# The opening of a hybrid attention encoder kernel: idle products first, half-size first loads, row scalings ahead of the squares, roots by square root and reciprocal

## The chip, the cores and the metric

The kernel runs on one core of a Trainium2 chip. The core has TensorE (PE, matrix products into PSUM), VectorE (DVE), ScalarE (ACT), GpSimd (POOL) and SyncE (SP), which here issues nearly all DMA transfers. Each engine takes its instructions in the order in which they were written to its queue and waits on semaphores for the others. The metric is the device time of one execution in microseconds (us); lower is better. The profile is one execution, recorded by the hardware; its span runs from the first to the last instruction.

## What is computed

One encoder layer is applied to 2048 prompt tokens and 512 sample tokens of width 1024, with 16 meta tokens ahead of each. What matters here is the beginning:

```python
def rms_norm(x, g):
    y = x32 * lax.rsqrt(jnp.mean(x32 * x32, axis=-1, keepdims=True) + RMS_EPS)
    return (y * g.astype(jnp.float32)).astype(x.dtype)

u = rms_norm(h, norm_g)
proj = u @ w_in                       # 1024 x 5376
qa, ka, va, za, qb, kb, vb, zb, ga, gb = jnp.split(proj, cuts, axis=-1)
# neighbourhood attention (a), windowed attention (b), gates, and
merged = jax.nn.sigmoid(ga) * y_a + jax.nn.sigmoid(gb) * y_b
return merged @ w_out                 # added to h, then a final rms_norm
```

Everything is float32. The kernel keeps that precision with three products of split operands: each operand is rounded to a high part (`fp32r`), the rest is the low part, and high x high, high x low and low x high are summed in PSUM (`mm3`, L146 to L148).

## The kernel before

The 2560 tokens are five windows of 512. Tokens lie along the free axis, the 1024 features along the 128 partitions in eight tiles. The opening projects the **last window** first, one weight tile (128 output features) at a time: 18 weight tiles in the list `firsts`, then the passes over pairs of windows follow. I call the 24 products (8 feature tiles x 3) of one weight tile a **group**; groups 1 to 4 make the queries of branch a, groups 5 to 8 those of branch b.

The projection needs only x times the norm's gain. The row factor, 1/sqrt(mean of squares), is a factor per token and is multiplied onto the group's result. So products can begin before the squares are summed. What the opening computes, by names that the profile shows:

- `wraw` is a weight tile as loaded, `wt` its high part (ACT, L207) and low part (VectorE, L208). Two buffers each.
- `xt` is a loaded pair of x tiles of the last window. `prep_last` scales it into the operand `u`: high part on ACT (L341), low part on VectorE (L342). It squares `xt` on ACT (L345) and sums the squares over the feature tiles into `rs` on VectorE (L347, L350). `xm` and `xms` are the same for the 16 meta tokens.
- `prep_last` is a generator. Its second part, the **row sums**, sums `rs` over the partitions with products against ones (`fin_v`, L368 and L369), takes the root (`rsqrt`, L151 to L164, an integer first guess and three Newton steps on VectorE) and writes it on a diagonal (`rs_dg`, L177). Its third part, the **spread**, turns the diagonal into a row factor on all partitions with products (`rs_rb`, L185), copied to `rs`.
- `prep_first` does the same for the first two windows (tiles `x`, squares `sq` at L426, sums `rsp` on POOL for one window, L428 and L431, and on VectorE for the other).
- `tq` and `evq` (L288, L253, L254) multiply a group's result by the row factor and split it; the query writes `qa<-evq` and `qb<-evq` go out by SP's queue. `zr` is a block of zeros that SP also writes out in between.

PE's and SP's order is that of the code (a manual schedule); ACT, VectorE and POOL are ordered by a scheduler, which may move instructions past each other, and the order is fixed when the program is built. `beside` runs the groups and counts the steps of each (a step is six products, four steps a group): the tuple `own` says after which steps the second and the third part of `prep_last` come, and the list `at` says after which steps `prep_first` goes on. A transfer that SP issues for `wraw` waits until the buffer's former tile has been split.

Of the kernel before, what the change touches and what calls it, by code (L numbers as in the profile page):

```python
# [9 lines left out]
F32 = mybir.dt.float32  # L10
# [85 lines left out]
def encoder_block(ctx: ExitStack, tc: tile.TileContext, xT, x_end, w_in, w_pa, w_pb, w_o, norm_g, final_g,  # L96
# [33 lines left out]
    ones = f32(ones_r)  # L130
    warm = const.tile([P, 1], F32, name="warm")
    nc.vector.memset(warm, 1.0)
    nc.scalar.activation(warm, warm, AF.Silu)
    ng = const.tile([P, KT], F32, name="ng")
    nc.scalar.dma_start(ng, norm_g)
    fg = const.tile([P, KT], F32, name="fg")
# [4 lines left out]
    def move(out, in_):  # L141
        last_move[0] = nc.sync.dma_start(*(f32(a) if a.dtype == F32R else a for a in (out, in_)))
        return last_move[0]
# [6 lines left out]
    def rsqrt(small, sq, m, nc_):  # L150

        ve, hv, r, t = (small.tile([P, 8], F32, tag=f"rs{i}", name=f"rs{i}")[:m, :nc_] for i in range(4))
        nc.vector.tensor_scalar(ve, sq, 1.0 / D_MODEL, EPS, ALU.mult, ALU.add)
        nc.vector.tensor_scalar(r.bitcast(I32), ve.bitcast(I32), 1, None, ALU.arith_shift_right)
        nc.vector.tensor_scalar(r.bitcast(I32), r.bitcast(I32), -1.0, float(0x5F3759DF), ALU.mult, ALU.add)
        nc.vector.tensor_scalar(hv, ve, -0.5, None, ALU.mult)
        for _ in range(3):
            if nc_ == 1:
                nc.vector.scalar_tensor_tensor(t, r, hv, r, ALU.mult, ALU.mult)
            else:  # L160
                nc.vector.tensor_mul(t, r, hv)
                nc.vector.tensor_mul(t, t, r)
            nc.vector.scalar_tensor_tensor(r, t, 1.5, r, ALU.add, ALU.mult)
        return r  # L164

    def sums(ssq, c0, m, nc_, psum, tag):
# [31 lines left out]
    def fetch_w(src):  # L198
        raw = wpool.tile([P, KT * P], F32, tag="wraw", name="wraw")
        if len(src.shape) == 3:  # L200
            move(raw.rearrange("p (a f) -> p a f", a=2), src.rearrange("a p f -> p a f"))
        else:
            move(raw, src)
        return raw
# [12 lines left out]
    class Weights:  # L217
# [16 lines left out]
        def next(self):  # L234
            i = self.i
            self.i += 1
            self.fetch(i + 2)
            self.split(i + 1)
            return self.wt.pop(i)
# [81 lines left out]

        return (up if i < 5 else uxp).tile(shape, F32R, tag=f"u{i}", name=name)

    def prep_last(meta):


        w = NWIN - 1
        uh, ul = (operand(i, [P, KT, PITCH], f"u4{i}") for i in (5, 6))
        us[w] = (uh, ul, us[w][2] if w in us else uxp.tile([P, UW + N_META], F32, tag="rs4", name="rs4")[:, :UW])
        rs = us[w][2]  # L330
        for k in range(0, KT, 2):
            rows = xT[k * P : (k + 2) * P]
            xt = ev.tile([P, 2, WTOK], F32, tag="ev", name="xt")
            move(xt, rows[:, w * WTOK : (w + 1) * WTOK].rearrange("(k p) t -> p k t", p=P))
            if meta and k == 0:
                xm = st.tile([P, KT, N_META], F32, tag="xm", name="xm", bufs=1)
                move(xm, xT[:, TOK:].rearrange("(k p) t -> p k t", p=P))
            for j in range(2):
                g = ng[:, k + j : k + j + 1]
                h = uh[:, k + j, :WTOK]  # L340
                nc.scalar.mul(h, xt[:, j, :], g)  # L341
                low[0] = nc.vector.scalar_tensor_tensor(ul[:, k + j, :WTOK], xt[:, j, :], g, f32(h), ALU.mult,  # L342
                                                        ALU.subtract).ins
            if meta:
                nc.scalar.activation(xt, xt, AF.Square)  # L345
                if k == 0:
                    nc.vector.tensor_add(rs[:, :WTOK], xt[:, 0, :], xt[:, 1, :])  # L347
                else:
                    for j in range(2):
                        nc.vector.tensor_add(rs[:, :WTOK], rs[:, :WTOK], xt[:, j, :])  # L350
        if not meta:
            return
        t = ev.tile([P, WTOK], F32, tag="t", name="xms", bufs=3)
        a, b = (t[:, i * P : (i + 1) * P].rearrange("p (k m) -> p k m", m=N_META) for i in range(2))
        nc.vector.tensor_mul(a, xm, ng[:, :, None].broadcast_to([P, KT, N_META]))
        mh, ml = uh[:, :, WTOK:UW], ul[:, :, WTOK:UW]
        nc.scalar.copy(mh, a)
        nc.vector.tensor_sub(ml, a, f32(mh))
        nc.scalar.activation(b, xm, AF.Square)
        for n in (4, 2):  # L360
            nc.vector.tensor_add(b[:, :n], b[:, :n], b[:, n : 2 * n])
        nc.vector.tensor_add(rs[:, WTOK:], b[:, 0], b[:, 1])
        yield
        sq = st.tile([P, 32], F32, tag="sq", name="sq", bufs=1)[:, :5]
        nc.vector.memset(sq, 1.0)
        v = ps_t.tile([P, WTOK], F32, tag="vt", name="fin_v")
        for c in range(4):
            nc.tensor.matmul(v[:, c : c + 1], rs[:, c * P : (c + 1) * P], ones[:, 0:1], start=True, stop=True)  # L368
        nc.tensor.matmul(v[:N_META, 4:5], rs[:, WTOK:], ones[:, 0:1], start=True, stop=True)  # L369
        nc.scalar.copy(sq[:, :4], v[:, :4])  # L370
        nc.scalar.copy(sq[:N_META, 4:5], v[:N_META, 4:5])
        r = rsqrt(uxp, sq, P, 5)
        dgs = [ev.tile([P, WTOK], F32, tag="t", name="rs_dg", bufs=3) for _ in range(2)]
        diagonal(dgs[0], r[:, :4], P)
        diagonal(dgs[1], r[:N_META, 4:5], N_META)
        yield
        for dg, c0, m, nc_ in (dgs[0], 0, P, 4), (dgs[1], WTOK, N_META, 1):
            nc.scalar.copy(rs[:, c0 : c0 + nc_ * m], spread(ps_t, "vt", dg, m, nc_)[:, : nc_ * m])
        yield
# [25 lines left out]
    def prep_first(sp, wa, loaded):  # L405
# [28 lines left out]
        for i in range(2):  # L434
            for c in range(4):
                nc.tensor.matmul(v[:, 4 * i + c : 4 * i + c + 1], rss[i][:, c * P : (c + 1) * P], ones[:, 0:1],
                                 start=True, stop=True)
        r = rsqrt(uxp, v[:, :8], P, 8)
        dgs = [ev.tile([P, WTOK], F32, tag="t", name="rs_dg", bufs=3) for _ in range(2)]
        for i in range(2):  # L440
            diagonal(dgs[i], r[:, 4 * i : 4 * i + 4], P)
# [557 lines left out]
    firsts = [*range(QA, KA), *range(QB, KB), *range(KA, ZA), KB, VB]  # L999
    rest = [f for f in range(GA) if f not in firsts]  # L1000

    def start_w(fs):
        raws = [fetch_w(w_in[f]) for f in fs[:1]]
        wts = [split_w(raws[0])]
        yield raws, wts
        raws.append(fetch_w(w_in[fs[1]]))
        raws.append(fetch_w(w_in[fs[2]]))
        yield
        wts.append(split_w(raws[1]))
        raws.append(fetch_w(w_in[fs[3]]))  # L1010
        yield
# [3 lines left out]
            pool = [pp.enter_context(tc.tile_pool(name=f"p{i}", bufs=1, reuse_waits="tile")) for i in range(3)]  # L1015
            return pairs(pool, wa, wa + 1, both, a, first.send(pool[2]), first, raw1, ahead, extra, opening)

    w0 = start_w(firsts)
    raws, wts = next(w0)
    own = prep_last(True)  # L1020
    next(own)
    with tc.tile_pool(name="sp", bufs=1, reuse_waits="tile") as sp:
        loaded = []
        steps = prep_first(sp, 0, loaded)
        next(w0)
        next(steps)
        next(w0)
        loaded.append(last_move[0])
        next(steps)
        zeros = zero_rows()  # L1030
        next(zeros)
        begun = beside(firsts, raws, wts, (own, (9, 14)), 0, steps, [2, 20, 27, *(28 + 27 * i // 10 for i in range(16))],
                       zeros)
    steps = [(0, 1), *((n, i) for n in range(1, KT) for i in (0, 1)), (KT, 0), (KT, 1), (KT, 2), (9, 1),
             *((j, i) for j in range(10, 18) for i in ((0, 2) if j % 2 == 0 else (1,)))]
# [777 lines left out]
```

## Time and profile before

| what | value |
|---|---|
| three runs | 1873.13, 1873.22, 1875.83 us; median 1873.22 |
| the profiled execution | 1874.68 us, span 1872.9 us |
| PE busy | 1851.8 us, 99% |
| VectorE, ACT, POOL busy | 70%, 61%, 42% |
| first product | 7.20 us after the span's start |
| mean granted TensorE clock | 0.999 |

The page's busy table gives each engine's share of the span. The table of waits says for which instruction of which engine an engine stood idle: total us, times, longest. A timeline row gives start, duration, engine, line, operation, what is written from what, its count and, in brackets, the idle time before it and what ended it. A row of a table of windows gives a stretch, its length, the busy time of PE, weight loads, VectorE, ACT and POOL with their instructions in brackets, the granted clock, the DMA engines' busy share and GB/s.

### The profile page before, as it was taken

What the parts mean: (1) busy time and instruction counts of PE and PEld (TensorE: products, weight loads), DVE (VectorE), ACT (ScalarE), POOL (GpSimd) and SP (SyncE); (2) the same over time, 40 slices, a digit from 0 to 9 for tenths busy, and PEclk for the clock granted to TensorE, in tenths of its full rate; (3) what the DMA queues carried; (4) which work ended last, traced back from release to release, by engine and by line L of the source; (5) the groups of instructions that cost most, each with busy time, mean ns of one, the idle gap of its engine ahead of it and who ended that gap; (6) DMA issues with size and microseconds to landing.
All of it is one profiled execution on the core that took longest, in us unless ns stands there. A gap on an engine that the chain in (4) does not pass through costs nothing. (4 is left out here: it accounts for less than half of the span.)

```text
span 1872.9 us, 29663 instructions
## 1 busy us (share of the span) xinstructions
PE 1851.8 (99%) x9755; PEld 1579.9 (84%) x9755; DVE 1317.6 (70%) x2914; ACT 1147.7 (61%) x2531; POOL 778.4 (42%) x599
## 2 busy tenths in 40 slices
PE   8999999999999999999999999999999999999998
PEld 6998888888888888888878888888888888888887
DVE  8986667556476556444457888878887887888874
ACT  6454444444365444444456797798789778878932
POOL 2015443323103232322324435647855865785420
PEclk9999999999999999999999999999999999999999
DMA  7665756645295677644259869968986998698473
GB/s 261 202 176 212 207 163 194 214 174 180 84 340 194 185 224 201 199 140 160 106 186 298 274 206 275 307 211 255 313 276 205 300 307 253 210 315 262 147 302 131
DMA packets 288145, 414.35 MB, mean 221 GB/s; under 512 B 117736, under 2 KB 162360, under 8 KB 286456
## 3 DMA queue, kind: packets, MB, share of 16 engines
q1 hardware_dynamic: 287704, 412.45, 68.9%
q8 instruction: 78, 1.28, 0.3%
q14 instruction: 75, 0.61, 0.1%
q10 hardware_dynamic: 288, 0.01, 0.0%
HBM read 303.46 MB, written 108.91 MB: 220 GB/s over the span
## 5 line engine op out<-in xcount | busy, mean ns | idle before, releaser
L208 POOL TENSOR_TENSOR wt<-wraw,wt 128x512 fp32r<-128x512 f32 x164 | 212.4, 1313 | 240.9 <-ACT wt L207 222.2
L868 PE MATMUL pa<-u,wt 128*128 128x512 f32 x1008 | 242.7, 389 | 0.2 <-DVE wt L208 0.2
L868 PE MATMUL pa<-u,x 128*128 128x512 f32 x984 | 236.5, 389 | 0.0
L207 ACT CAST wt<-wraw 128x512 fp32r<-128x512 f32 x312 | 177.8, 619 | 76.2 <-DMA wraw<-in_w_in_dram 29.8
L868 PEld LDWEIGHTS pa<-u,wt 128*128 128x128 f32 x1008 | 188.9, 188 | 39.8 <-DVE wt L208 0.6
L868 PEld LDWEIGHTS pa<-u,x 128*128 128x128 f32 x984 | 184.6, 188 | 38.4
L837 POOL TENSOR_TENSOR s<-wraw,raw 128x512 f32<-128x512 f32 x40 | 58.3, 1458 | 276.7 <-DVE x L208 276.7
L146 PE MATMUL mm<-u,wt 128*128 128x512 f32 (+2 forms) x416 | 150.2, 361 | 7.2 <-ACT u L341 7.2
L147 PE MATMUL mm<-u,wt 128*128 128x512 f32 (+2 forms) x416 | 146.8, 353 | 0.2 <-DVE u L342 0.2
L148 PE MATMUL mm<-u,wt 128*128 128x512 f32 (+2 forms) x416 | 146.7, 353 | 0.0
L208 DVE TENSOR_TENSOR wt<-wraw,wt 128x512 fp32r<-128x512 f32 x148 | 103.8, 738 | 53.5 <-ACT wt L207 53.4
L868 PE MATMUL pe<-u,wt 128*128 128x512 f32 x504 | 121.3, 390 | 0.0
L868 PE MATMUL pc<-u,wt 128*128 128x512 f32 x504 | 121.1, 389 | 0.0
L868 PE MATMUL pe<-u,x 128*128 128x512 f32 x480 | 115.3, 389 | 0.0
L842 POOL TENSOR_TENSOR s<-wraw,s 128x512 f32<-128x512 f32 x42 | 56.6, 1349 | 137.7 <-DVE wt L208 137.7
L868 PEld LDWEIGHTS pc<-u,wt 128*128 128x128 f32 x504 | 94.6, 188 | 19.6
L868 PEld LDWEIGHTS pe<-u,wt 128*128 128x128 f32 x504 | 94.4, 188 | 19.6
L1174 ACT CAST ph<-tp 128x384 fp32r<-128x384 f32 (+6 forms) x160 | 81.7, 510 | 42.9 <-PE tp L1171 41.4
L1175 DVE TENSOR_TENSOR pl<-tp,ph 128x384 fp32r<-128x384 f32 (+6 forms) x160 | 94.8, 593 | 18.3 <-ACT ph L1174 15.5
L146 PE MATMUL pso<-mh,wt 128*128 128x512 f32 x256 | 107.5, 420 | 0.0
L868 PEld LDWEIGHTS pe<-u,x 128*128 128x128 f32 x480 | 90.1, 188 | 18.7
L1070 DVE CUSTOM_DVE_ANT_0 s<-s,ba 128x384 f32<-128x384 f32 (+5 forms) x160 | 86.6, 541 | 24.0 <-PE s L1148 23.5
(274 smaller groups left out, 5029.1 us busy)
## 6 DMA issues: line engine op xcount, KB each, us to landing
wraw<-in_w_in_dram SPq DMA_DIRECT2D x86, 512.0 KB
raw<-in_w_in_dram SPq DMA_DIRECT2D x40, 512.0 KB
q<-qa SPq DMA_DIRECT2D x40, 512.0 KB
wraw<-in_w_o_dram SPq DMA_DIRECT2D x32, 512.0 KB
kbt<-kb SPq DMA_DIRECT2D x32, 384.0 KB
qa<-evq SPq DMA_DIRECT2D x20, 512.0 KB
qb<-evq SPq DMA_DIRECT2D x20, 512.0 KB
ka<-evk SPq DMA_DIRECT2D x20, 512.0 KB
```

The lines of the kernel that those rows point to most:

```text
L146: nc.tensor.matmul(ps, wh, uh, start=first, stop=False)
L147: nc.tensor.matmul(ps, wh, ul, start=False, stop=False)
L148: nc.tensor.matmul(ps, wl, uh, start=False, stop=last)
L207: high[0] = nc.scalar.copy(h, r).ins
L208: low[0] = (eng or lo_eng[0]).tensor_sub(l, r, f32(h)).ins
L837: eng.tensor_sub(s3, a11, a21)
L842: eng.tensor_sub(s4, a12, s2)
L868: nc.tensor.matmul(ps, wt[:, a, s], u[:, b, kk, :], start=first and kk == 0 and i == 0, stop=kk == 3 and i == 2, skip_group_check=True)
L1070: nc.vector.tensor_tensor_reduce(s[:, :n], s[:, :n], bias, -1.0, 3.0e38, ALU.add, ALU.min, nm)
L1174: nc.scalar.copy(ph_[:kb, a], tb)
L1175: nc.vector.tensor_sub(pl_[:kb, a], tb, f32(ph_[:kb, a]))
```

## The change

Four things are changed in the first microseconds, and nothing else in the program:

1. **Idle products.** VectorE fills a 128x512 tile `wide` with ones, and PE multiplies it with itself ten times into a PSUM tile that nobody reads, ahead of the first product.
2. **First loads.** The first weight tile is loaded and split in two halves, each x pair of the last window in two single tiles, and the first x pair is issued between the two halves. The load of `xm` moves behind the second and third weight tiles.
3. **Scalings first.** All eight scalings of the last window stand ahead of its four squares; squares and sums come behind the split of the second weight tile. The row sums move from after step 9 to after step 10, the spread from after step 14 to after step 16, the row sums of the first windows from step 20 to step 22.
4. **Roots.** Both roots of the opening come from `root`: a square root on ACT, a reciprocal on VectorE and one Newton step, instead of the integer guess with three steps. ACT loads the table for the square root at the start instead of SiLU's, and SiLU's before its first use.

```diff
-    nc.scalar.activation(warm, warm, AF.Silu)
+    nc.scalar.activation(warm, warm, AF.Sqrt)
+    eps = const.tile([P, 1], F32, name="eps")
+    nc.vector.memset(eps, EPS)
...
+    def root(small, sq, nc_):
+        s, hv, r, t = (small.tile([P, 8], F32, tag=f"rs{i}", name=f"rs{i}")[:, :nc_] for i in range(4))
+        nc.scalar.activation(s, sq, AF.Sqrt, bias=eps, scale=1.0 / D_MODEL)
+        nc.vector.tensor_scalar(hv, sq, -0.5 / D_MODEL, -0.5 * EPS, ALU.mult, ALU.add)
+        nc.vector.reciprocal(r, s)
+        nc.vector.tensor_mul(t, r, hv)
+        nc.vector.tensor_mul(t, t, r)
+        nc.vector.scalar_tensor_tensor(r, t, 1.5, r, ALU.add, ALU.mult)
+        return r
...
-    def prep_last(meta):
+    def prep_last(meta, side=None):
...
+        xts = []
         for k in range(0, KT, 2):
             rows = xT[k * P : (k + 2) * P]
             xt = ev.tile([P, 2, WTOK], F32, tag="ev", name="xt")
-            move(xt, rows[:, w * WTOK : (w + 1) * WTOK].rearrange("(k p) t -> p k t", p=P))
-            if meta and k == 0:
-                xm = st.tile([P, KT, N_META], F32, tag="xm", name="xm", bufs=1)
-                move(xm, xT[:, TOK:].rearrange("(k p) t -> p k t", p=P))
+            xts.append(xt)
+            src = rows[:, w * WTOK : (w + 1) * WTOK].rearrange("(k p) t -> p k t", p=P)
+            if meta:
+                for j in range(2):
+                    move(xt[:, j], src[:, j])
+            else:
+                move(xt, src)
+            if k == 0 and side is not None:
+                next(side)
             for j in range(2):
...
-            if meta:
+        if not meta:
+            return
+        yield
+        xm = st.tile([P, KT, N_META], F32, tag="xm", name="xm", bufs=1)
+        move(xm, xT[:, TOK:].rearrange("(k p) t -> p k t", p=P))
+        yield
+        with tc.issue_after(high[0]), tc.issue_after(low[0]):
+            for k, xt in enumerate(xts):
                 nc.scalar.activation(xt, xt, AF.Square)
...
-        r = rsqrt(uxp, sq, P, 5)
+        r = root(uxp, sq, 5)
...
-        r = rsqrt(uxp, v[:, :8], P, 8)
+        r = root(uxp, v[:, :8], 8)
...
+        if halves:
+            raws = [wpool.tile([P, KT * P], F32, tag="wraw", name="wraw")]
+            wts = [wpool.tile([P, 2, KT * P], F32R, tag="wt", name="wt")]
+            for c in (slice(0, 4 * P), slice(4 * P, KT * P)):
+                move(raws[0][:, c], w_in[fs[0]][:, c])
+                split_part(wts[0][:, 0, c], wts[0][:, 1, c], raws[0][:, c])
+                yield raws, wts
...
-    w0 = start_w(firsts)
+    wide = ev.tile([P, WTOK], F32R, tag="t", name="wide", bufs=3)
+    nc.vector.memset(f32(wide), 1.0)
+    idle = ps_t.tile([P, WTOK], F32, tag="vt", name="idle")
+    for _ in range(10):
+        nc.tensor.matmul(idle, wide[:, :P], wide, start=True, stop=True)
+    w0 = start_w(firsts, True)
     raws, wts = next(w0)
-    own = prep_last(True)
+    own = prep_last(True, w0)
     next(own)
...
-        begun = beside(firsts, raws, wts, (own, (9, 14)), 0, steps, [2, 20, 27, *(28 + 27 * i // 10 for i in range(16))],
+        begun = beside(firsts, raws, wts, (own, (10, 16)), 0, steps, [2, 22, 27, *(28 + 27 * i // 10 for i in range(16))],
```

`issue_after` only orders the instructions of one engine behind the one named; it adds no wait between engines.

The order of SP's queue at the start (`wraw` weights, `xt` the last window, `xm` meta tokens, `x_350` a tile of the first windows; 128x512 is 0.26 MB), before:

```order
L142 DMA wraw<-in_w_in_dram 128x1024
L142 DMA xt<-in_xT_dram 128x2x512
L142 DMA xm<-in_xT_dram 128x8x16
L142 DMA xt<-in_xT_dram 128x2x512 x3
L142 DMA wraw<-in_w_in_dram 128x1024 x2
L142 DMA x_350<-in_xT_dram 128x2x512 x2
```

And with the change:

```order
L144 DMA wraw<-in_w_in_dram 128x512
L144 DMA xt<-in_xT_dram 128x512 x2
L144 DMA wraw<-in_w_in_dram 128x512
L144 DMA xt<-in_xT_dram 128x512 x6
L144 DMA wraw<-in_w_in_dram 128x1024 x2
L144 DMA xm<-in_xT_dram 128x8x16
L144 DMA x_351<-in_xT_dram 128x2x512 x2
```

Half a weight tile and two x tiles stand first, and the small load of the meta tokens has gone behind three weight tiles.

ACT from its first cast to the squares of the first windows, before (`sq<-x_351` is the square whose sum is POOL's first add):

```order
L207 CAST wt<-wraw 128x512 x2
L341 ACTIVATE u_292<-xt,ng 128x512 x2
L359 ACTIVATE xms<-xm 128x128
L357 CAST u_292<-xms 128x8x16
L341 ACTIVATE u_292<-xt,ng 128x512 x2
L345 ACTIVATE xt<-xt 128x1024
L341 ACTIVATE u_292<-xt,ng 128x512 x2
L345 ACTIVATE xt<-xt 128x1024
L341 ACTIVATE u_292<-xt,ng 128x512 x2
L207 CAST wt<-wraw 128x512 x2
L345 ACTIVATE xt<-xt 128x1024 x2
L207 CAST wt<-wraw 128x512 x2
```

With the change, to the same point and one row further (`x_352` is now the name of that tile):

```order
L220 CAST wt<-wraw 128x512
L360 ACTIVATE u_305<-xt,ng 128x512 x2
L220 CAST wt<-wraw 128x512
L360 ACTIVATE u_305<-xt,ng 128x512 x6
L220 CAST wt<-wraw 128x512 x2
L371 ACTIVATE xt<-xt 128x1024 x4
L220 CAST wt<-wraw 128x512 x2
L383 ACTIVATE xms<-xm 128x128
L381 CAST u_305<-xms 128x8x16
L450 ACTIVATE sq<-x_352 128x1024 x2
```

The four squares moved from between the scalings to behind the second weight tile's casts, and the meta tokens' pieces from the front to the end.

VectorE from the split of the second weight tile to that of the fourth, before (`rs_294` holds the sums of squares):

```order
L208 TENSOR_TENSOR wt<-wraw,wt 128x512 x2
L350 TENSOR_TENSOR rs_294<-rs_294,xt 128x512 x2
L208 TENSOR_TENSOR wt<-wraw,wt 128x512 x2
L350 TENSOR_TENSOR rs_294<-rs_294,xt 128x512 x2
L208 TENSOR_TENSOR wt<-wraw,wt 128x512 x2
```

And with the change (`rs_307`):

```order
L221 TENSOR_TENSOR wt<-wraw,wt 128x512 x2
L379 TENSOR_TENSOR xms<-xm,ng 128x128
L728 MEMSET zr 128x128
L373 TENSOR_TENSOR rs_307<-xt 128x512
L376 TENSOR_TENSOR rs_307<-rs_307,xt 128x512 x4
L221 TENSOR_TENSOR wt<-wraw,wt 128x512 x2
L376 TENSOR_TENSOR rs_307<-rs_307,xt 128x512
L385 TENSOR_TENSOR xms<-xms 128x64
L382 TENSOR_TENSOR u_306<-xms,u_305 128x8x16
L376 TENSOR_TENSOR rs_307<-rs_307,xt 128x512
L385 TENSOR_TENSOR xms<-xms 128x32
L386 TENSOR_TENSOR rs_307<-xms 128x16
```

All seven adds now stand behind the second weight tile's split, where four stood, and the meta tokens' pieces are between the last two.

More of the change, by code (lines that the diff above doesn't have):

```diff
@@ L350, in prep_last @@
                         nc.vector.tensor_add(rs[:, :WTOK], rs[:, :WTOK], xt[:, j, :])
-        if not meta:
-            return
         t = ev.tile([P, WTOK], F32, tag="t", name="xms", bufs=3)
@@ L1000, in encoder_block, with start_w @@
     rest = [f for f in range(GA) if f not in firsts]
[L1002 to L1005, printed above, removed]
+    def start_w(fs, halves=False):
+        if halves:
[5 more added lines that the diff above has]
+                yield raws, wts
+        else:
+            raws = [fetch_w(w_in[f]) for f in fs[:1]]
+            wts = [split_w(raws[0])]
+            yield raws, wts
         raws.append(fetch_w(w_in[fs[1]]))
@@ L1025, in encoder_block @@
         next(w0)
+        next(own)
         next(steps)
         next(w0)
+        next(own)
         loaded.append(last_move[0])
```

## The prediction

> **What bounds the kernel now.** I read the page's busy table first, then the waits of TensorE (PE) over the whole span, and then the timelines of the first 60 us engine by engine. The first two:
>
> ```profile
> span 1872.9 us, 29663 instructions
> PE 1851.8 (99%) x9755; PEld 1579.9 (84%) x9755; DVE 1317.6 (70%) x2914; ACT 1147.7 (61%) x2531; POOL 778.4 (42%) x599
> ...
> PE mm L146 <- ACT u L341: 7.2, 1, 7.2
> ...
> PE rs_rb L185 <- DVE rs_dg L177: 0.9, 1, 0.9
> ```
>
> PE is busy for 99% of the span. A microsecond that PE gains early is a microsecond at the end, unless a later wait takes it back. The change can touch two of these waits: 7.2 us before the first product, and 0.9 us before the spread of the first root. A third cost is no wait at all; only PE's timeline shows it:
>
> ```profile
> 7.20 0.80 PE L146 MATMUL mm<-u,wt 128*128 128x512 f32 x1 [7.20 <-ACT u L341]
> ...
> 11.98 0.63 PE L147 MATMUL mm<-u,wt 128*128 128x512 f32 x1
> 12.41 0.46 PE L148 MATMUL mm<-u,wt 128*128 128x512 f32 x1
> ...
> 12.94 0.40 PE L147 MATMUL mm<-u,wt 128*128 128x512 f32 x1
> 13.17 0.39 PE L148 MATMUL mm<-u,wt 128*128 128x512 f32 x1
> ...
> 15.89 0.40 PE L146 MATMUL mm<-u,wt 128*128 128x512 f32 x1
> ...
> 21.37 0.39 PE L146 MATMUL mm<-u,wt 128*128 128x512 f32 x1
> ...
> 22.73 0.95 PE L368 MATMUL fin_v<-ones,rs 128*128 128x1 f32 x8
> 23.74 0.50 PE L146 MATMUL mm<-u,wt 128*128 128x512 f32 x1
> ...
> 31.69 1.48 PE L185 MATMUL rs_rb<-rs_dg,ones 128*128 128x128 f32 x10 [0.86 <-DVE rs_dg L177]
> ```
>
> Starts lie 0.43 us apart until 12.4 and 0.23 us apart from 12.9, so the first 12 products run at half speed. A group (one weight tile, 24 products) is 24 x 0.228 = 5.47 us at full speed. Group 1 runs from 7.20 to 15.89, group 2 to 21.37; the row sums (fin_v) cut group 3 at 22.73, after 6 products, and the spread (rs_rb) cuts group 4 after 12.
>
> **The loads and groups 1 and 2.** Rows of ACT, of the stretch from 10 to 20 us (last columns: DMA share, GB/s), and of VectorE (DVE):
>
> ```profile
> 4.43 1.14 ACT L207 CAST wt<-wraw 128x512 fp32r<-128x512 f32 x2 [1.77 <-DMA wraw<-in_w_in_dram]
> 6.42 1.34 ACT L341 ACTIVATE u<-xt,ng 128x512 fp32r<-128x512 f32 x2 [0.85 <-DMA xt<-in_xT_dram]
> ...
> 10.00:20.00 10.00, 9.83 (x38) 7.62 (x37) 9.80 (x15) 9.83 (x14) 1.15 (x1) 1.00 1.03 384
> ...
> 0.88 0.17 DVE L636 MEMSET km<- 128x128 f32 x1
> ...
> 14.52 0.74 DVE L342 SCALAR_TENSOR_TENSOR u<-xt,ng,u 128x512 fp32r<-128x512 f32 x1
> ```
>
> The first 0.5 MB is usable at 4.43, and at 384 GB/s each further 0.26 MB takes 0.69 us. In the new order the first half weight tile is there at 3.75, x tiles at 4.43 and 5.1, the other half at 5.8, six x tiles until 9.9, the second weight tile at 11.3, the third at 12.7. An x tile needs ACT (1.34 for two, 0.7 for one) and then VectorE (0.74): the last low part is ready at 9.9 + 0.7 + 0.75 = 11.4. Two products remain, so group 1 ends at 12.0.
>
> The ten idle products begin near 1.4, behind a memset that I put at 0.5 from the 0.17 for a quarter of its width, and last 10 x 0.43 = 4.3 us, to 5.7; the first low part is ready at 5.9. When the clock then opens matters little: three cold products take 1.28 us, and even if it opened only at 8, two x tiles would be done and the other six would end at 12.2. If idle products did not count at all, the clock would open 5.2 us (7.20 to 12.4) after 5.7, group 1 would end near 13.7, and the next limit below would hide that.
>
> Group 2 waits 0.15 us for the low part of its weights (11.3, cast 0.6, subtract 0.65) and ends at 12.0 + 0.15 + 5.47 = 17.6, against 21.37. So PE is **3.75 us ahead** there. That is not yet the gain.
>
> **The row sums, where part of it goes.** All eight scalings now stand ahead of the four squares, and so the sums come later. Rows of ACT, VectorE and GpSimd (POOL):
>
> ```profile
> 13.74 1.13 ACT L207 CAST wt<-wraw 128x512 fp32r<-128x512 f32 x2
> 14.77 2.01 ACT L345 ACTIVATE xt<-xt 128x1024 f32<-128x1024 f32 x2
> 17.71 2.19 ACT L426 ACTIVATE sq<-x 128x1024 f32<-128x1024 f32 x2
> ...
> 16.39 1.41 DVE L350 TENSOR_TENSOR rs<-rs,xt 128x512 f32<-128x512 f32 x2
> 17.72 1.29 DVE L208 TENSOR_TENSOR wt<-wraw,wt 128x512 fp32r<-128x512 f32 x2
> 18.92 3.48 DVE L350 TENSOR_TENSOR rs<-rs,xt 128x512 f32<-128x512 f32 x2
> ...
> 18.85 1.31 POOL L428 TENSOR_TENSOR rsp<-sq 128x512 f32<-128x512 f32 x1 [17.55 <-ACT sq L426]
> 20.23 3.31 POOL L431 TENSOR_TENSOR rsp<-rsp,sq 128x512 f32<-128x512 f32 x2
> ```
>
> ACT, new order: the second weights from 11.3 (1.03, as from 13.74 to 14.77), four squares from 12.3 (0.96 each, so done at 16.2), the third weights (1.03), two small pieces for the meta tokens (0.45), and the first square of x_352 from 17.7 to 18.75. So POOL starts at about **18.8**, as it does now. VectorE: first add at 13.5; a pair for each of the next two squares (1.33 each), to 17.1; third weights, 18.3; sixth add, 18.95; then a small add and the low part of the meta tokens; only then the seventh. Undisturbed it would end at 20.1, and PE comes to the row sums, now 12 products into group 3, at 17.6 + 2.73 = 20.35.
>
> It is not undisturbed. Two adds that take 1.41 us alone took 3.48 beside POOL's: the two engines take turns. So the small add that is due at 18.95 waits out POOL's first add (about 20.1), the meta piece slips in behind it, and the seventh add waits out POOL's second, to 21.6; with its own 0.65 it ends at **22.25**. PE waits 1.9 us. The last small sum for the meta tokens may lose a further turn, which costs PE 0 to 0.5 us; I take 0.3.
>
> So PE goes on at 22.25 + 1.0 (the sums' own time, 22.73 to 23.74) + 0.3 = 23.55, with 12 products left, where it now goes on at 23.74 with 18 left. Bounds: 22.0 without a collision (0.5 us of wait and the late meta sum), 24.85 with one more turn lost.
>
> **The roots and the spread.** Thirteen small VectorE instructions become five and one on ACT, twice. In the rows that follow, VectorE's first root runs beside POOL's adds, and then come the second root's surroundings on VectorE, SP's queue, ACT and PE:
>
> ```profile
> 25.82 1.15 DVE L161 TENSOR_TENSOR rs<-rs,rs 128x5 f32<-128x5 f32 x1
> 27.00 0.17 DVE L162 TENSOR_TENSOR rs<-rs,rs 128x5 f32<-128x5 f32 x1
> ...
> 40.30 5.20 SPq L142 DMA_DIRECT2D qa<-evq  x4
> 45.55 0.65 SPq L142 DMA_DIRECT2D wraw<-in_w_in_dram  x1
> ...
> 50.76 1.14 ACT L207 CAST wt<-wraw 128x512 fp32r<-128x512 f32 x2 [6.93 <-DMA wraw<-in_w_in_dram]
> 51.98 1.28 DVE L208 TENSOR_TENSOR wt<-wraw,wt 128x512 fp32r<-128x512 f32 x2
> ...
> 41.40 1.84 PE L436 MATMUL fin_v<-ones,rsp 128*128 128x1 f32 x16
> 52.77 1.95 PE L185 MATMUL rs_rb<-rs_dg,ones 128*128 128x128 f32 x16
> ```
>
> The first spread now stands at the end of group 4, 12 products later: 23.55 + 2.74 + 5.47 = 31.76. Its diagonal came at 31.69 and comes earlier now, since the sums are as late as before and eight steps of 0.17 to 1.15 us are gone. So the 0.86 us wait goes. No row shows a square root or a reciprocal of this size; taken as 0.17 or as 1.15 each they fit into the same room.
>
> **Group 5 is the place to take the sum**: it starts at 31.69 + 1.48 + 12 x 0.228 = 35.9 now, and at 31.76 + 1.48 = 33.24 after the change. The gain is **2.66 us**; 4.2 without a collision, 1.36 with one more turn lost.
>
> **Behind it** the cover is thinner. The tightest piece is the weight tile of group 8. SP issues it behind the four query writes (45.55), it lands at 50.76, its first low part is ready at 52.6, and PE needs that at 35.9 + 3 x 5.47 + 1.84 + 1.95 + 0.45 = 56.55: 3.9 us of cover. With PE 2.7 us ahead and the chain at its old time, 1.3 remain. I cost it at nothing, and one for one beyond 1.3. The new table load stands before the first SiLU:
>
> ```profile
> 1.16 1.28 ACT L133 ACT_TABLE_LOAD   x1 [1.16 <-PEq L1798]
> ...
> 302.33 0.63 ACT L300 ACTIVATE eva<-eva 128x512 f32<-128x512 f32 x1 [2.93 <-DVE eva L288]
> ...
> 40.00:50.00 10.00, 10.00 (x53) 8.54 (x53) 8.24 (x24) 2.18 (x4) 0.00 (x0) 1.00 0.72 261
> 1325.00:1350.00 25.00, 24.61 (x149) 20.94 (x147) 20.19 (x52) 18.65 (x41) 21.12 (x18) 1.00 1.03 320
> 1336.18 9.38 DMA q<-qa
> ```
>
> It takes 1.28 us where ACT idles 2.93: nothing, or 1.28 if that idle time were gone.
>
> **The time.** Span 1872.9 - 2.66 = 1870.2. That execution took 1874.68, 1.78 more than its span; the median of the three runs is 1873.22, and I take the gain off that: **1870.6 us**.
>
> **The rivals.**
> 1. No collision: the meta pieces and the seventh add get in before POOL's turns. For it: the margin is 0.15 us (18.8 against 18.95). Against it: 0.6 us of add is left when POOL is due. Gain 3.9 to 4.6 (no wait at all): 1868.9.
> 2. One turn more is lost: small add, meta piece and seventh add each wait out one POOL add, and the sum is ready at 23.55. Against it: of the small root steps beside POOL only every second one waited (1.15, then 0.17). Gain 1.4: 1871.8. [...]
> 3. Given back later: from 1325 to 1350 the DMA share is 1.03, and transfers take 9.38 us; if they cannot follow, a PE that is ahead waits. Against it: that chain begins at a VectorE release, which moves too. Gain 0 to 1: 1872.7.
> 4. Slower, by SP's queue: the fourth query write needs a VectorE step that now stands behind the second root's reciprocal, and so behind ACT's square root. If the weight tiles of groups 8 to 10 each land 9.4 us after their issue, as at 1336, PE waits about 3, 2 and 2 us: 7 - 2.7 = 4.3 slower, 1877.5. It decides from 3.9 us of lateness. Against it: the DMA share there is 0.72.
>
> **Chances.** Forecast 0.45, rival 1 0.32, rival 2 0.09, rival 3 0.07, rival 4 0.07. About 0.2% (3.75 us) is what a measurement of this kernel can tell from no change. Faster by more than that: nearly all of rival 1 and a tenth of the forecast, 0.35. Slower: rival 4, 0.07. The rest, 0.58, is the same. The range reaches over rivals 1 to 3: 1868.2 to 1873.4.
>
> **What would show it.** Right: group 1 ends near 12.0 and group 2 near 17.6; PE idles 1.5 to 2.5 us before fin_v, released by the adds into rs; one or two of the last adds into rs take over 1 us beside POOL's first; the spread waits for nothing; PE has no new wait between 33 and 60. Wrong: no idle time before fin_v (rival 1); products still 0.43 us apart beyond 9 us; a PE wait for wt in groups 5 to 10 (rival 4).

## The result: 0.5% slower

The changed kernel takes **1885.47 us** (median of five, 1883.81 to 1888.06) beside 1875.5 us for the kernel before on the same chip: ratio 1.0053, 95% interval 1.0039 to 1.0067. The forecast was 1870.6 in a range from 1868.2 to 1873.4. The profiled execution took 1885.74 us. The page of the changed kernel:

```profile
span 1884.0 us, 29682 instructions
PE 1869.1 (99%) x9765; PEld 1584.3 (84%) x9765; DVE 1320.3 (70%) x2900; ACT 1149.3 (61%) x2534; POOL 781.4 (41%) x599
```

PE is busy for 99% of the span, as before, though with 17 us more work (1869.1 against 1851.8) in ten more products (x9765 against x9755). Those ten are the idle products, 4.6 us; the other 12.7 us are no new instructions. The span is 11.1 us longer, and the longest waits hold nothing that explains it:

```profile
PE idle L1054 <- DVE wide L1051: 1.5, 1, 1.5
PE tp L1210 <- DVE pr L1127: 1.4, 1, 1.4
PE fin_v L392 <- DVE rs L376: 1.4, 1, 1.4
```

**The opening.** PE's timeline of the changed kernel, with the first products of groups and those at which the spacing (start to start) changes:

```profile
1.50 4.63 PE L1054 MATMUL idle<-wide 128*128 128x512 f32 x10 [1.50 <-DVE wide L1051]
5.94 0.63 PE L148 MATMUL mm<-u,wt 128*128 128x512 f32 x1
...
13.29 0.39 PE L148 MATMUL mm<-u,wt 128*128 128x512 f32 x1
...
18.92 0.40 PE L148 MATMUL mm<-u,wt 128*128 128x512 f32 x1
...
21.48 0.40 PE L150 MATMUL mm<-u,wt 128*128 128x512 f32 x1
23.29 1.33 PE L392 MATMUL fin_v<-ones,rs 128*128 128x1 f32 x8 [1.41 <-DVE rs L376]
...
24.81 0.79 PE L148 MATMUL mm<-u,wt 128*128 128x512 f32 x1
25.40 0.63 PE L149 MATMUL mm<-u,wt 128*128 128x512 f32 x1
...
30.52 0.50 PE L149 MATMUL mm<-u,wt 128*128 128x512 f32 x1
...
35.99 1.37 PE L198 MATMUL rs_rb<-rs_dg,ones 128*128 128x128 f32 x10
37.29 0.50 PE L148 MATMUL mm<-u,wt 128*128 128x512 f32 x1
```

The rows at 13.29 and 18.92 are the first products of groups 2 and 3, so groups 1 and 2 end there (before: 15.89 and 21.37). Then PE waits for the sums, and behind them products start 0.43 us apart: 13 spacings from 24.81 to 30.52, twice what they take elsewhere. A table of windows of the same stretch, whose last three columns are the granted clock, the DMA share and GB/s, shows the clock at 0.50 from 24 to 30 us.

```profile
20.00:24.00 4.00, 2.59 (x15) 1.88 (x14) 4.00 (x5) 1.60 (x3) 3.84 (x3) 0.99 1.05 409
24.00:27.00 3.00, 2.95 (x11) 2.46 (x11) 2.83 (x10) 2.05 (x5) 0.82 (x2) 0.50 0.89 307
27.00:30.00 3.00, 3.00 (x8) 2.32 (x8) 3.00 (x3) 2.24 (x3) 2.84 (x3) 0.50 0.79 224
```

Group 5 starts at 37.29; before, its row stands at 35.96. So the opening loses 1.3 us where 2.66 were to be gained.

**Everything behind it.** The larger loss lies elsewhere. For a line, a view lists its products: count, then shortest, median and longest duration in ns, and the start of the first and of the last. Before, and changed (the first `pa<-u,wt` opens the passes over the windows, the last stands 11 us ahead of their end):

```profile
L868 PE MATMUL pa<-u,wt x1008: 387/389/501, 122.3 to 959.5; 128*128 128x512 f32 x168
L868 PE MATMUL pc<-u,wt x504: 389/389/389, 125.1 to 951.4; 128*128 128x512 f32 x168
L868 PE MATMUL pe<-u,x x480: 389/389/397, 145.3 to 956.8; 128*128 128x512 f32 x160
```

```profile
L892 PE MATMUL pa<-u,wt x1008: 387/389/501, 124.1 to 970.2; 128*128 128x512 f32 x168
L892 PE MATMUL pc<-u,wt x504: 389/389/389, 126.8 to 961.8; 128*128 128x512 f32 x168
L892 PE MATMUL pe<-u,x x480: 395/396/401, 147.1 to 967.4; 128*128 128x512 f32 x160
```

The passes begin 1.8 us later, and from the first of these products to the last it takes 846.1 us instead of 837.2: **8.9 us**, in a part of the program that the diff does not touch. Behind that point hardly anything more is lost (1884.0 - 970.2 = 913.8; before 913.4), and 1.8 + 8.9 + 0.4 are the 11.1 us. Not one of the 480 `pe<-u,x` is as fast as their median was before: the median is 396 ns against 389. About half of `pa<-u,x` are slow too (498 of 984 take 394 ns or more, 11 of 984 before; by the code, those that read `u5`), while `pc<-u,wt` did not change (389). The slow ones read the tiles `u5` and `u6`, which lie where the last window's operand lies. The opening's products read that place too, and their starts lie 0.235 us apart (13.29 to 18.92 is 24 of them) instead of 0.228 (15.89 to 21.37). From start to start, `pe<-u,x` takes 3.2 us more in all, `pa<-u,x` 3.3 and 192 products of eight later groups of the last window 1.3: most of the 8.9 us.

What can slow single products there? The change allocates one more constant, `eps`, four bytes wide, which takes 32. As the built programs place their tiles, all that is allocated behind it, the weight tiles and the passes' own operands among it, lies 32 bytes further up in each partition (the first `wt` at 25856 instead of 25824). The last window's operand is allocated from the other end and stays (190176). Before, the two lay a multiple of 256 bytes apart (190176 - 25824 is 642 x 256).

### The profile page after: what moved, and what is told of

Its sections match the earlier page's. It is cut to its first block, busy times and chain, and to the rows that moved or that the text cites. A ratio compares the mean times of both kernels' runs of the same rounds, so it can differ in the third digit from the quotient of the medians.

```text
span 1884.0 us, 29682 instructions
## 1 busy us (share of the span) xinstructions
PE 1869.1 (99%) x9765; PEld 1584.3 (84%) x9765; DVE 1320.3 (70%) x2900; ACT 1149.3 (61%) x2534; POOL 781.4 (41%) x599
## 3 DMA queue, kind: packets, MB, share of 16 engines
q8 instruction: 78, 1.28, 0.3%
```

## Experiments on the shift

Theory A: the 32 bytes are the cause. Rival B: one of the four parts of the change is. Eight kernels set the two sides, weights and last window's operand, at different distances. The table gives the distance by what is left of it over multiples of 256 bytes (modulo 256), the median of `pe<-u,x`, and the passes' length from the first to the last `pa<-u,wt`:

| kernel | weights moved | last window's operand moved | distance modulo 256 | `pe<-u,x` ns | passes us | ratio to before (95%) |
|---|---|---|---|---|---|---|
| before | 0 | 0 | 0 | 389 | 837.2 | 1 |
| changed | +32 | 0 | 224 | 396 | 846.1 | 1.0053 (1.0039 to 1.0067) |
| a_noshift | 0 | 0 | 0 | 389 | 837.2 | 0.9994 (0.9983 to 1.0005) |
| b_left32 | +32 | 0 | 224 | 396 | 846.3 | 1.0043 (1.0028 to 1.0059) |
| b_left64 | +64 | 0 | 192 | 394 | 845.8 | 1.0027 (1.0018 to 1.0036) |
| b_both32 | +32 | -32 | 192 | 394 | 846.0 | 1.0033 (1.0021 to 1.0045) |
| b_left128 | +128 | 0 | 128 | 395 | 845.2 | 1.0047 (1.0033 to 1.0060) |
| b_left256 | +256 | 0 | 0 | 389 | 837.4 | 0.9996 (0.9985 to 1.0007) |
| b_down32 | -32 | -32 | 0 | 389 | 837.8 | 0.9981 (0.9970 to 0.9992) |
| a_pad256 | +256 | 0 | 0 | 389 | 840.0 | 1.0000 (0.9987 to 1.0012) |

**The changed kernel without the shift (a_noshift)**, 1875.63 us:

```diff
-    warm = const.tile([P, 1], F32, name="warm")
-    eps = const.tile([P, 1], F32, name="eps")
+    wide2 = const.tile([P, 2], F32, name="warm")
+    warm, eps = wide2[:, 0:1], wide2[:, 1:2]
```

> The changed kernel, with its new constant (the epsilon of the roots) put into the second column of the tile `warm`, which takes 32 bytes of a partition either way. No other tile then moves against the kernel before; everything else of the change stays. Theory A (the 32 bytes that the constant took moved the weight tiles and the operands of the passes against the last window's operand, and products that read one of each became 0.2333 us apart instead of 0.2275): products of the opening 0.2275 apart, `pe<-u,x` 389 ns again instead of 396, median 1875 to 1877, that is 9 to 10 us off the change's 1885.5. Rival B (one of the four parts of the change itself slows the products or costs the time elsewhere): 1884 to 1887, products still 0.2333 apart.

```profile
L892 PE MATMUL pa<-u,wt x1008: 387/389/499, 122.1 to 959.3; 128*128 128x512 f32 x168
L892 PE MATMUL pe<-u,x x480: 389/389/397, 145.1 to 956.6; 128*128 128x512 f32 x160
```

Theory A's numbers. With all of the change in place the products are as fast as before, and so is the kernel.

**The shift alone (b_left32, b_left64, b_left128, b_left256)**: the kernel before with an unread tile of 8, 16, 32 or 64 columns.

```diff
     nc.scalar.activation(warm, warm, AF.Silu)
+    pad = const.tile([P, 8], F32, name="pad")
+    nc.vector.memset(pad, EPS)
```

> The kernel before with nothing but a constant tile of 32 bytes a partition, written once and read by nobody, where the change put its constant. Theory A: 1884 to 1887 (1875.5 + 9 to 11), `pe<-u,x` 396 ns, products of the opening 0.2333 apart. Rival B: 1875.5, within 1, and 0.2275 apart.

> The same with 64 bytes. If theory A is a matter of position modulo 64 bytes: 1875.5, within 1, `pe<-u,x` 389 ns. If any move of these tiles costs the time, or if the extra instruction does: 1884 to 1887 as with 32 bytes. Rival B: 1875.5.

The row of b_left32, then that of b_left64:

```profile
L870 PE MATMUL pe<-u,x x480: 395/396/401, 146.0 to 966.3; 128*128 128x512 f32 x160
```

```profile
L870 PE MATMUL pe<-u,x x480: 390/394/394, 144.6 to 964.6; 128*128 128x512 f32 x160
```

An unread tile of 32 bytes costs the kernel before what the change cost. My modulus of 64 was wrong: 64 bytes cost nearly as much.

**Both sides moved (b_both32, b_down32).** In b_both32 the row factor's tile is 32 bytes longer too, which pushes the last window's operand down; in b_down32 `warm` goes to the other end, which moves both sides down.

```diff
-    ... uxp.tile([P, UW + N_META], F32, tag="rs4", name="rs4")
+    ... uxp.tile([P, UW + N_META + 8], F32, tag="rs4", name="rs4")
```

```diff
+    cr = ctx.enter_context(tc.tile_pool(name="cr", bufs=1, side="right"))
-    warm = const.tile([P, 1], F32, name="warm")
+    warm = cr.tile([P, 1], F32, name="warm")
```

> The 32 bytes of the unread tile, and the row factor's tile of the last window longer by 32 bytes, which moves the last window's operand down by 32 bytes. If what counts is the distance between the two operands of a product (theory A, relative): 1875.5, within 1, `pe<-u,x` 389 ns. If it is the place of the weights and of the passes' operands by itself (theory A, absolute): 1884 to 1887. Rival B: 1875.5.

> The kernel before with the tile `warm` (32 bytes) moved from the low end of the partitions to the high end: all weight tiles and operands of the passes move down by 32 bytes, and the last window's operand and everything beside it moves down by 32 bytes as well. The distance of any two of them is that of the kernel before. If the distance counts (32 bytes one way in b_left32, 64 in b_left64 and in b_both32, which moved the two sides apart in opposite directions, all slow): 1876.8, within 1.5, `pe<-u,x` 389 ns. If any move from the places of before costs the time: 1883 to 1887, `pe<-u,x` 394 to 396 ns.

First b_both32, then b_down32:

```profile
L870 PE MATMUL pe<-u,x x480: 393/394/396, 144.3 to 964.3; 128*128 128x512 f32 x160
```

```profile
L869 PE MATMUL pe<-u,x x480: 388/389/397, 147.0 to 958.7; 128*128 128x512 f32 x160
```

b_both32 was slow, which had been the sign for the place of the weights by itself; but it moved the sides apart by 64 bytes, not back together, and its median is that of b_left64 (394). b_down32, which moves everything and keeps the distance, has 389. So **the distance counts**, not the place. The weights' own place is no rival: in the changed kernel `pc<-u,wt` reads the moved weight tiles with an operand that moved with them, in 389 ns, and the opening's products read the same weight tiles with the last window's operand, which stayed, and are slow. b_down32 came out 0.2% below before, with every engine's instructions in the order of before. In its profiled execution the part behind the passes is 3.0 us shorter (910.4 us against 913.4), but that part lies anywhere from 910.2 to 917.8 us over the profiles of all these kernels; why b_down32 is faster stays open.

**The modulus (b_left256, b_left128).**

> The kernel before with an unread constant tile of 256 bytes. If the distance counts modulo 128 or 256 bytes: 1876.8, within 1.5, `pe<-u,x` 389 ns. If modulo 512 or more, or if any move costs the time: 1883 to 1887, 394 to 396 ns.

> The kernel before with an unread constant tile of 128 bytes. If the distance between the operands counts modulo 128 bytes: 1875.8, within 1.5, `pe<-u,x` 389 ns. If modulo 256: 1880 to 1887, 392 to 396 ns.

First b_left256, then b_left128:

```profile
L870 PE MATMUL pe<-u,x x480: 389/389/397, 144.8 to 956.4; 128*128 128x512 f32 x160
```

```profile
L870 PE MATMUL pe<-u,x x480: 391/395/399, 146.0 to 965.6; 128*128 128x512 f32 x160
```

Fast at 256, slow at 128. The four kernels with only a `pad` differ in nothing but its size, and every engine's instructions stand in one order in all four.

**The changed kernel with a longer constant (a_pad256)**, 1876.64 us: a change of one number, and the same order of instructions on all engines as in the changed kernel.

```diff
-    eps = const.tile([P, 1], F32, name="eps")
+    eps = const.tile([P, 64], F32, name="eps")[:, :1]
```

> The changed kernel with its constant tile made 256 bytes long instead of 32, of which the first four are used; every engine's instructions stand in the same order as in the changed kernel. If the distance between the last window's operand and the weights counts modulo 256 bytes (theory A as the shifted kernels left it): `pe<-u,x` 389 ns instead of 396, the 9 to 11 us back, a time as a_noshift's, ratio to before 0.999 to 1.0005. If the loss in the changed kernel has another cause than in the shifted kernels: 1.004 to 1.006, 396 ns.

```profile
L892 PE MATMUL pe<-u,x x480: 389/389/397, 145.7 to 959.6; 128*128 128x512 f32 x160
```

389 ns and ratio 1.0000: without the shift's effect on the products no loss against before is left. (Its profiled execution was the longest of its twelve, 1881.93 us, with waits late in the program; the 840.0 us in the table hold 1.5 us of waits.)

## Experiments on the opening

Without the shift the change is worth nothing that can be measured, where 2.66 us were forecast. The interval of a_noshift (down to 0.9983) would still allow 2.66 us; its trace does not, since group 5 starts 0.36 us ahead of before (35.60 against 35.96). PE does this:

```profile
22.92 1.05 PE L392 MATMUL fin_v<-ones,rs 128*128 128x1 f32 x8 [1.67 <-DVE rs L376]
24.30 0.20 PE L393 MATMUL fin_v<-ones,rs 128*16 128x1 f32 x2 [0.33 <-DVE rs L386]
24.43 0.79 PE L148 MATMUL mm<-u,wt 128*128 128x512 f32 x1
...
27.58 0.48 PE L149 MATMUL mm<-u,wt 128*128 128x512 f32 x1
...
35.60 0.50 PE L148 MATMUL mm<-u,wt 128*128 128x512 f32 x1
```

Seven products at half speed (the granted clock is 0.55 from 24.0 to 27.5 us), group 5 at 35.60. The kernels that follow stand on a_noshift unless told otherwise.

**Sums two steps later (a_late)**, 1877.1 us, ratio 1.0009 (0.9996 to 1.0022):

```diff
-... (own, (10, 16)), 0, steps, [2, 22, 27, ...
+... (own, (12, 17)), 0, steps, [2, 22, 27, ...
```

> The changed kernel without the shift (the epsilon in `warm`), and the row sums of the last window two steps (12 products) later, the spread one step later: `own` is (12, 17) instead of (10, 16). Theory C (PE waits 1.67 + 0.33 us for the sums, and after that wait and the single-column sums 7 products run at 0.43 instead of 0.23 us apart, 1.6 us with the first; 14 such products in the changed kernel itself): no wait at fin_v, no half-speed product behind it, group 5 starts near 32.0 instead of 35.6, span 1868 to 1868.5, median about 1872.0 if a_noshift is 1875.6. Rival D (that lead is given back at a later wait, for weights or at a PSUM buffer): group 5 near 32 but span above 1870.5, with a new wait between 32 and 130 us. Rival E (the wait for the last adds follows, since VectorE's order changes with it): a wait of 1 us or more stays at fin_v.

Rival D. PE came to the sums without a wait or half speed, and then stood at group 5's low weights; PE, and VectorE with what it waited for:

```profile
33.45 0.50 PE L150 MATMUL mm<-u,wt 128*128 128x512 f32 x1 [2.51 <-DVE wt L221]
...
34.55 2.44 PE L198 MATMUL rs_rb<-rs_dg,ones 128*128 128x128 f32 x10
36.92 0.80 PE L148 MATMUL mm<-u,wt 128*128 128x512 f32 x1
```

```profile
31.65 1.75 DVE L221 TENSOR_TENSOR wt<-wraw,wt 128x512 fp32r<-128x512 f32 x1
```

That subtract takes 1.75 us beside POOL's adds (26.49 to 32.85), where the next one, at 33.92, takes 0.68; it stands behind the adds into `rsp`. Here is a floor, in this order of VectorE's instructions: the third product of group 5, the first with low weights, waits for that subtract, which ends at 33.4. And behind the 2.51 us the clock closed again (0.53 from 34.5 to 38.0 us; the spread took 2.44 us instead of 1.37).

**No idle products (a_noidle)**, 1873.08 us, ratio 0.9988 (0.9976 to 1.0000):

```diff
-    wide = ev.tile([P, WTOK], F32R, tag="t", name="wide", bufs=3)
-    nc.vector.memset(f32(wide), 1.0)
-    idle = ps_t.tile([P, WTOK], F32, tag="vt", name="idle")
-    for _ in range(10):
-        nc.tensor.matmul(idle, wide[:, :P], wide, start=True, stop=True)
```

> The changed kernel without the shift and without the ten idle products and the tile they read. If the idle products open the clock early (first products at 0.43 us until 6.9 us, then at 0.23): without them the first ten or twelve products lie 0.43 us apart, group 1 ends 1.0 to 2.0 us later than 12.9, the wait before fin_v (1.67 us) shrinks by as much, and the time is that of a_noshift within 1 us, since PE only arrives earlier at a wait. If PE's clock closes later because of the idle products' window: the half-speed products behind fin_v are gone too, and the span is 1.0 to 1.6 shorter, near 1870.4.

```profile
5.68 0.79 PE L148 MATMUL mm<-u,wt 128*128 128x512 f32 x1 [5.68 <-ACT u L360]
...
22.34 1.05 PE L392 MATMUL fin_v<-ones,rs 128*128 128x1 f32 x8 [0.47 <-DVE rs L376]
...
31.78 1.37 PE L198 MATMUL rs_rb<-rs_dg,ones 128*128 128x128 f32 x10
33.08 0.50 PE L148 MATMUL mm<-u,wt 128*128 128x512 f32 x1
```

No half speed behind the sums (the granted clock is 1.00 over the first 60 us), and group 5 at 33.08, where the forecast had 33.24; the passes begin at 119.6, 2.7 us ahead of before. It is not a clean cut: without the idle products the scheduler also put the meta pieces ahead of POOL's first add, and so the sums came at 22.3 instead of 22.9.

**Idle products alone (b_idle)**, the kernel before with those five lines added: 1874.89 us, ratio 0.9992 (0.9981 to 1.0002).

> The kernel before with the ten idle products and the tile they read, and nothing else of the change. The last add into rs ends at 22.4 (18.92 + 3.48) in the kernel before and PE comes to the sums at 22.7. If idle products open the clock and only bring PE earlier to the same adds: products 0.23 us apart from about 8 us on instead of 12.9, a new wait of 1 to 2 us before fin_v, group 5 no earlier than 35.6, and the time within 1.5 us of before; where the clock closes behind that wait, 7 to 14 products at 0.43 us and 1.4 to 2.8 us more. If they pay by themselves: no wait at fin_v, group 5 near 33.5 to 34, the time 2 us below before.

```profile
11.78 0.50 PE L147 MATMUL mm<-u,wt 128*128 128x512 f32 x1 [0.29 <-DVE u L342]
...
22.61 0.94 PE L368 MATMUL fin_v<-ones,rs 128*128 128x1 f32 x8
```

They are worth 0.12 us at the sums (22.61 against 22.73) and nothing at group 5 (35.94 against 35.96). The wait is not at fin_v, as I had expected, but ahead of the products themselves: at full speed PE waits for x tiles (1.14 us for the first, then four times 0.3).

**PE kept busy at its wait (a_keep)**, 1877.16 us, ratio 1.0004 (0.9995 to 1.0014): seven more idle products ahead of the row sums.

```diff
+        idle = ps_t.tile([P, WTOK], F32, tag="vt", name="idle")
+        for _ in range(7):
+            nc.tensor.matmul(idle, wide[:, :P], wide, start=True, stop=True)
         v = ps_t.tile([P, WTOK], F32, tag="vt", name="fin_v")
```

> The changed kernel without the shift, with seven more idle products (7 x 0.228 = 1.6 us) just ahead of the row sums, where PE waited 1.67 us. If the wait and the single-column sums close the clock: the products behind the sums are 0.23 us apart at once (7 of them were 0.43 apart), group 5 starts near 34.0 instead of 35.6, and the time is 1 to 2 us below a_noshift, near 1874. If the half speed has another cause (the sums alone, or a fixed time after the start): 7 products or more at 0.43 us as before, group 5 at 35.6.

```profile
21.62 1.75 PE L392 MATMUL idle<-wide 128*128 128x512 f32 x7
...
24.96 0.50 PE L148 MATMUL mm<-u,wt 128*128 128x512 f32 x1
...
34.59 0.50 PE L148 MATMUL mm<-u,wt 128*128 128x512 f32 x1
```

The half speed is gone (the granted clock is 1.00 over the first 60 us) and group 5 starts 1.0 us earlier than in a_noshift (34.0 was expected). The median does not show it (1.0 us is 0.05%).

**Old roots (a_oldroot)**, on a_noidle, both roots in their old form and SiLU's table first again: 1875.25 us, ratio 0.9988 (0.9976 to 1.0000).

```diff
-        r = root(uxp, sq, 5)
+        r = rsqrt(uxp, sq, P, 5)
```

> The changed kernel without the shift and without idle products, and with both roots of the opening in their old form (integer guess, three Newton steps, no square root on ACT, one table load fewer). Prediction's step: the old root's eight further steps lie on the way to the diagonal, which then comes 1.5 to 4 us later than 29.4, and PE, which reaches the spread at 31.78, waits 0 to 1.5 us there. If the root is off the path: spread within 0.3 of 31.8, and 1873 as a_noidle. If the square root and its table loads cost anything further on: the time is below a_noidle's 1873.1 by 1 or more.

```profile
32.72 1.48 PE L198 MATMUL rs_rb<-rs_dg,ones 128*128 128x128 f32 x10 [0.73 <-DVE rs_dg L190]
```

The spread starts 0.94 us later, 0.73 of it a wait for the diagonal: the new root is worth about that in the trace, and too little to show in the time.

**A version that beats both (a_best)**: a_noidle with both constants in one tile at the other end, as `warm` in b_down32. 1872.14 us, ratio 0.9979 (0.9967 to 0.9991):

```diff
+    cr = ctx.enter_context(tc.tile_pool(name="cr", bufs=1, side="right"))
-    wide2 = const.tile([P, 2], F32, name="warm")
+    wide2 = cr.tile([P, 2], F32, name="warm")
```

> The changed kernel without idle products, and with the two constants in one 32-byte tile at the high end of the partitions (as `warm` in b_down32, which took 1871.99). The distances are those of the kernel before. If only the distances count: as a_noidle, 1873.1 within 1. If something in b_down32's place was faster by itself (1872.0 against 1875.8): 1869 to 1870.

```profile
23.15 1.05 PE L393 MATMUL fin_v<-ones,rs 128*128 128x1 f32 x8 [1.51 <-DVE rs L377]
...
24.26 0.50 PE L149 MATMUL mm<-u,wt 128*128 128x512 f32 x1
```

0.2% faster than before. It fits the first case (1873.1 within 1) and is 2 us over the second; its interval overlaps that of a_noidle, so the place of the constants is not shown to be worth anything. In this execution a wait of 1.51 us did **not** close the clock (1.00 from 20 to 30 us).

## Why the prediction was wrong, point by point

- **"Group 5 is the place to take the sum"**: this step failed. It assumed that a product takes 0.228 us whatever the change does, and that a lead at group 5 reaches the end. The change moved tiles by 32 bytes, and the products that read the last window's place took 7 ns more: that is most of the 8.9 us lost between 124 and 970. The front part says that nothing else in the program was changed; that holds for its instructions, not for the places of its tiles. None of the rivals had this, since all were looked for in the order of the instructions.
- **"PE waits 1.9 us. ... So PE goes on at 23.55"**: the mechanism was right, a term was missing. PE came to the sums at 21.7 instead of 20.35, waited 1.41 us (1.67 in a_noshift) where 1.9 were forecast, and went on at 24.81 instead of 23.55: 1.04 us because the last add came at 23.23 instead of 22.25, and 0.2 more for the sums. Not foreseen was that the clock closes behind it (0.50 from 24 to 30 us): the 13 spacings from 24.81 to 30.52 took 5.71 us instead of 2.96, 2.75 us. With 0.2 us for the slower products up to the spread and a spread 0.2 us shorter, these make up the 4.05 us between 33.24 and 37.29.
- **VectorE's turns with POOL**: right in the times. POOL's first add runs from 19.70 to 21.27, and the small add, begun at 20.03, takes 1.32 us, to 21.35; POOL's next two run from 21.35 to 24.36, and the seventh add takes 1.75 beside them, where the sixth, at 19.43, took 0.68. That one waits out the other, as the prediction put it, is a reading of these times. VectorE's rows:

```profile
20.03 1.32 DVE L385 TENSOR_TENSOR xms<-xms 128x64 f32<-128x64 f32 x1
21.28 0.28 DVE L382 TENSOR_TENSOR u<-xms,u 128x128 fp32r<-128x128 f32 x1
21.48 1.75 DVE L376 TENSOR_TENSOR rs<-rs,xt 128x512 f32<-128x512 f32 x1
23.16 1.25 DVE L385 TENSOR_TENSOR xms<-xms 128x32 f32<-128x32 f32 x1
```

  It ran 1 us later than worked out (the small add began at 20.03 instead of 18.95), and so did the loads: ACT began the casts of the first half weight tile at 4.17 (3.75 in the prediction) and of the second tile at 12.28 (11.3). The prediction took 384 GB/s, a row of 10 to 20 us, from the start; from 4 to 8 us the DMA engines moved 334 GB/s. The last small add lost the further turn that I had priced at 0 to 0.5 us; it cost PE nothing in the changed kernel and 0.33 us in a_noshift. Rival 1 is out, since there is a collision. Rival 2's time for the sum, 23.55, came near 23.23, though by that 1 us and not by one more turn.
- **Loads and groups 1 and 2**: near. Group 1 ended at 13.3 for 12.0, group 2 at 18.9 for 17.6, of which 0.3 us is the slower product.
- **"When the clock then opens matters little"**: right, and more so than I used it. b_idle puts the idle products at 0.12 us. I should have concluded that PE is then only earlier at a wait.
- **Roots and spread**: right. The wait of 0.86 us is gone; a_oldroot brings 0.73 back.
- **Table load at nothing**: right. It takes 1.28 us and stands where ACT idled 2.93 (2.92 now), and PE has no wait there.
- **Rival 3**: not seen; the part behind the passes is 0.4 us longer, within what that part varies. **Rival 4**: false. PE has no wait for `wt` in groups 5 to 10. The cover on VectorE was thinner than that of SP's queue: a_late runs into it at 33.45.

Without the shift the working still does not hold as it stands. In a_noshift group 5 starts at 35.60 and not at 33.24: the sums began at 22.92 instead of 22.25, took 0.2 us longer, and seven products at half speed cost 1.6 us. So what fails there are the time of the sums, by 0.7 us, and the half speed, which the prediction did not have. a_noidle comes to 33.08, and 1873.08 there against 1875.84 is 2.8 us, at the edge of what the runs can tell. That this is the forecast number is in part luck: a_noidle leaves out the idle products, VectorE's order differs, and PE waits 0.47 us at the sums instead of 1.9.

## What to carry to other kernels

A new tile, even of four bytes, moves all that is allocated behind it (by 32 bytes here, and products went from 389 to 396 ns): compare the places of the matmul operands of both programs before costing a change by its instructions, and look at the mean duration of the products that the change does not touch. An engine that is brought early to a wait gains nothing by it (b_idle: 0.12 us at the sums), and PE's clock can close there, as it did here behind 1.41 us (0.50 for 6.83 us), so price the wait with what may follow it. A lead is worth what the next late producer allows, here VectorE's low weights.

## What the runs showed of the hardware

- A product of 128x512 (`fp32r` operands) that reads its operand at one end of the partitions, with weights at the other, took 389 ns (median of `pe<-u,x`) in the five kernels of the table whose distance is a multiple of 256 bytes: before, a_noshift, b_left256, b_down32 and a_pad256. It took 394 to 396 ns in the five others, at 32 (changed, b_left32), 64 (b_left64, b_both32) or 128 bytes off (b_left128). The loads of weights take 188 ns in the kernel before and in the changed one. What slows the products is not shown.
- The clock closed behind 1.41 us (changed), 1.67 and 0.33 (a_noshift), 1.65 and 0.33 (a_pad256) and 2.51 us (a_late) of PE's waiting, all but the last with single-column sums behind it, and not behind 1.51 us in a_best or 0.47 in a_noidle. The half speed lasted 13, 7 and 8 products in the first three. In b_down32 the granted clock averaged 0.97 over the first 60 us, though the longest wait listed for PE there, behind the 7.0 us before the first product, is 0.5 us, at the row sums of the first windows. So the length of the wait does not decide by itself.
- In the changed kernel's profile the granted clock was full for 17.07 us from its first opening, half for 6.83, and then full for 1850.02; before, it was full for 1856.85 us from its first opening. These are 5, 2, 542 and 544 times 3.413 us. In the last 3.41 us before the clock closed (20.50 to 23.91), the products that start there, counted by columns (0.2275 us for 512), fill 1.14 us. In every other stretch of that length at full clock, laid end to end from the first opening up to 1840 us, they fill at least 1.60 us in this profile and 1.38 in that of the kernel before. This is one closing in one profile: it shows no limit, and no run set out to test one.
